# A hybrid trunk of two layers: where the dense blocks and the gates steps of its expert sub-layer are issued

## The chip, the cores and the metric

The kernel runs on one core of a Trainium2 chip. The metric is the device time of one execution in microseconds (us), of which the median over the runs is taken. Within the core, TensorE (PE in the trace, its weight loads PEld) multiplies matrices, VectorE (DVE) and ScalarE (ACT) work on tiles in the on-chip memories, GpSimd (POOL) does the same and issues the gathers of table rows, and SyncE (SP) issues all other transfers. Each engine has its own queue and works it off in order; an instruction waits until what it reads is there and its buffer is free.

## The reference

Two layers over 512 latent tokens and 256 context tokens of width 1024. Each layer is a token mixer (pooling, two kinds of scan, Fourier mixing) and then an expert sub-layer of the PEER kind, each followed by a residual sum and a LayerNorm. Only the expert sub-layer of the latent tokens is touched:

```python
q = (hb @ wq).reshape(t, PEER_HEADS, 2, PEER_DQ // 2)
s = jnp.einsum('thsd,hskd->thsk', q, sub_keys).astype(jnp.float32)
v1, i1 = lax.top_k(s[:, :, 0], PEER_TOPK)
v2, i2 = lax.top_k(s[:, :, 1], PEER_TOPK)
cand = (v1[..., :, None] + v2[..., None, :]).reshape(t, PEER_HEADS, PEER_TOPK * PEER_TOPK)
cid = (i1[..., :, None] * PEER_NKEYS + i2[..., None, :]).reshape(t, PEER_HEADS, PEER_TOPK * PEER_TOPK)
best, pos = lax.top_k(cand, PEER_TOPK)
eid = jnp.take_along_axis(cid, pos, axis=-1)
gate = jax.nn.softmax(best, axis=-1)
act = jax.nn.gelu(jnp.einsum('td,thkd->thk', hb, u_tab[eid]).astype(jnp.float32), approximate=False)
return jnp.einsum('thk,thkd->td', (gate * act).astype(hb.dtype), v_tab[eid])
```

Every token picks 16 of 16384 experts in each of 8 heads by two searches of 16 among 128 keys and one among their sums.

## The kernel before

**Two ways to the same sum.** The 512 latent tokens are four tiles of 128. For tile 3 (`gx`, "the gather") the picked rows of the tables u and v are fetched one per token: 128 turns, each one indirect DMA of 512 KB on POOL's queue (`gat<-in_u`) and one dot product on VectorE (`gat<-gat,hb`), then 128 turns with v, where VectorE adds each row, weighted, to `gacc`. A generator hands out these turns (257 with the last store), and the loops around it decide how many stand beside each piece of other work. It has four `gat` buffers (`GAT = 4`).

For tiles 0 to 2 (`ND = 3`) it is dense: all 16384 experts are applied to all 384 tokens, in 128 chunks of 128 experts, and the results are weighted with a gate matrix that is zero almost everywhere.

**A dense block** (`u_chunk`, L1670) is one chunk of u: SP loads `du` (512 KB), ACT rounds it to `dh`, the remainder `dl` is a subtraction on POOL for chunks below `UN = 48` and on VectorE for the others, TensorE does 24 products of 128x384, ACT takes the Gelu (`da`), and SP stores it to `acts` (192 KB). `du` has three buffers, `dh` and `dl` two. The last 40 chunks are done later, so 88 blocks are handed out by the generator `dense_u`.

**A gates step** (`gates_all`, L1625) makes the gate matrix for 16 tokens; there are 24. VectorE compares `it` (the transposed indices) with a row of numbers (`B`, and `A` twice multiplied with the gate `gp`), TensorE does 32 products `ps<-A,B` a step later, ACT copies them out, partly to `W` and partly through `wst` to DRAM (`rest`, 704 KB).

**The order of the work.** `peer_front` (L1766) computes the scores and searches of all four tiles and then, tile by tile (3, 0, 1, 2), the look-ups: `topk` (L1509) turns positions into expert numbers by comparing and adding up (`oh`, `sel`), all on VectorE. For a dense tile `dense_in` (L1613) has TensorE transpose the two indices and the gate and VectorE store them in `it` and `gp`. Between these pieces `fill` runs dense blocks at a lower priority: one per tile in each of the 8 score units (`FD = 1`, 32 in all) and `FT = 6` behind each tile's look-ups (24). A scheduler then orders each engine's queue by dependences and priority.

After `peer_front` a loop in `run` hands out the other blocks of `dense_u`, each followed by a gates step and `GU` gather turns (2). Then 40 blocks of `dense_uv` (u and v of a chunk together, 2 or 3 gather turns each) and 88 of `dense_v` (6 turns in 7 blocks), then the gather turns that are left and the residuals of the tiles. In layer 0 the context tiles' own gather ends during the look-ups of the latent tiles.

**Lines.** All engine calls go through one recorder, so every instruction has line L149; the tiles' names tell them apart.

Of the kernel before, what the change touches and what calls it, by code (L numbers as in the profile page):

```python
# [50 lines left out]
UN = 48  # L51
VO = 3
DV = 3
FT = 6
UO = 64
FD = 1
GV = (1,1,1,0,1,1,1)
GU = (2,)
GF = (2,3)
GAT = 4  # L60
M1 = ((16,12,9),(18,13,10))
# [122 lines left out]
class K:  # L184
# [1310 lines left out]
    def lookup(self, oh, tab, wide=False):  # L1495


        nc = self.nc
        t = self.oh()
        nc.vector.tensor_tensor(t, oh, tab[:, :, None, :].to_broadcast([128, 8, 16, 16]), op=OP.mult)  # L1500
        o = self.oh((128, 8, 16, 8), F32) if wide else t
        nc.vector.tensor_add(o[:, :, :, :8], t[:, :, :, :8], t[:, :, :, 8:])
        for n in (4, 2):
            nc.vector.tensor_add(o[:, :, :, :n], o[:, :, :, :n], o[:, :, :, n:2 * n])
        e = self.sm((128, 8, 16), "sel", 3)
        nc.vector.tensor_add(e, o[:, :, :, 0], o[:, :, :, 1])
        return e

    def topk(self, tk):  # L1509

        nc = self.nc
        ix, v, best, pos = tk

        gate = self.sm((128, 8, 16), "gate", 2)
        nc.vector.tensor_tensor(gate, best, best[:, :, 0:1].to_broadcast([128, 8, 16]), op=OP.subtract)
        nc.scalar.activation(gate, gate, AF.Exp)
        den = self.t([128, 8], "den", 2)
        nc.vector.tensor_reduce(den, gate, axis=AX.X, op=OP.add)
        nc.vector.reciprocal(den, den)
        nc.vector.tensor_tensor(gate, gate, den[:, :, None].to_broadcast([128, 8, 16]), op=OP.mult)  # L1520

        ib = self.sm((128, 8, 2, 16), "ib", 2, BF)
        nc.vector.tensor_copy(ib, ix)
        pb = self.sm((128, 8, 16), "pb", 2, BF)
        nc.vector.tensor_copy(pb, pos)
        d1 = self.sm((128, 8, 16), "d1", 2, BF)
        nc.vector.tensor_copy(d1[:, :, 0:1], ib[:, :, 0, 0:1])
        nc.vector.tensor_sub(d1[:, :, 1:], ib[:, :, 0, 1:], ib[:, :, 0, :15])
        shape = [128, 8, 16, 16]
        i16, p0, dp = (t[:, None, :].to_broadcast([128, 8, 16]) for t in self.tab)  # L1530
        ge = self.oh()
        nc.vector.tensor_tensor(ge, pb[:, :, :, None].to_broadcast(shape), p0[:, :, None, :].to_broadcast(shape),
                                op=OP.is_ge)
        e1 = self.lookup(ge, d1, True)
        st = self.lookup(ge, dp)
        nc.vector.tensor_sub(pb, pb, st)
        eq = self.oh()
        nc.vector.tensor_tensor(eq, pb[:, :, :, None].to_broadcast(shape), i16[:, :, None, :].to_broadcast(shape),
                                op=OP.is_equal)
        return gate, e1, self.lookup(eq, ib[:, :, 1, :])  # L1540
# [225 lines left out]
    def peer_front(self, l, x, fm, s, h, order, dense=None, n=0, m=0):  # L1766


        NT = len(x)

        self.lo_pool = True
        tk = [self.topk_tiles() for _ in range(NT)]

        def fn(u, S):
            for i in order:
                self.topk_head(u, S[i], tk[i])
                self.fill(n)
        self.peer_scores(l, h, NT, fn)
        self.lo_pool = False
        gg = []  # L1780
        for i in order:
            with self.section() as sec:
                top = self.topk(tk[i])
                if dense is not None and i < ND:
                    self.dense_in(i, top, *dense)
                else:
                    gg.append((i, self.gather_in(l, *top)))
            self.fill(m)
            if gg and (dense is None and len(gg) == NT or dense is not None and len(gg) == 1 and i == gg[0][0]):
                with self.section(sec):  # L1790
                    rows = [self.bcast_row(fm, g, s, 1.0) for g in (3, 4)]
                    gg = [(i, (self.h_tokens(x[i], rows),) + g) for i, g in gg]
        return [g for _, g in gg]

    def run(self):
# [5 lines left out]
        for l in range(L):  # L1801
# [7 lines left out]
            with ExitStack() as mix:  # L1809
# [44 lines left out]
                with self.phase("m2", **(dict(s2=M2X[0], xs2=M2X[1]) if last else dict(s2=M2, s4=3, xs2=M2Y))):  # L1854
# [8 lines left out]
                    late = []  # L1863
# [30 lines left out]
            with self.phase("fx", s2=4, s4=2, x4=2):  # L1894
                self.add(gu)
                gx = self.peer_front(l, x1, fm, 0, hT, (3, 0, 1, 2), (it, gp), FD, FT)
                self.fillers.clear()
            gen = self.gather(l, gx, [accx])
            with self.area("wk", side="right") as wk:

                W = [self.gate_tile(j, wk) for j in range(2)]
                with self.phase("wp"):
                    self.iota = self.t((128, 128, 2), "iota", 1, F16)
                    self.nc.vector.tensor_copy(self.iota, self.iota1[:, :, None].to_broadcast([128, 128, 2]))
                    gs = self.gates_all(it, gp, W, rest)
                    more = True
                    k = 0
                    go = Order(self, UO)
                    while more:
                        with go.main():  # L1910
                            more = next(gu, self) is not self
                        k += 1
                        with go.side():
                            next(gs, None)
                        self.beside(go, GU[k % len(GU)], gen)
                    self.run_all(gs)
                with self.area("vv", side="right") as vv:
                    acc = [[self.pa() if 2 * b + q < PA else self.p() for q in range(2)] for b in range(ND)]
                    go = Order(self, VO)
                    gates = self.gate_blocks(go, W, rest, wk)  # L1920
                    self.dense_uv(l, hT, hu, acc, go, gates, vv, gen)
                    dd.close()

                    def made():
                        if not last:
                            at = self.tc.cur_priority
                            self.tc.cur_priority += RP
                            with self.phase("rc", s2=6, s4=3, ld=3):
                                self.residual(c1, c2, self.spilled(accs), l, fm, 5, 1, 1.0, 2)
                            self.tc.cur_priority = at  # L1930
                    with self.area("aa", side="right") as aa:
                        self.dense_v(l, acts, acc, go, gates, vv, aa, gen, made)
                        self.run_all(gen)
                        with self.phase("rg", s2=6, s4=3, ld=3):
                            self.residual(x1[ND:], x2[ND:], self.spilled([accx]), l, fm, 5, 0, 1.0, 2)
# [133 lines left out]
```

## Time and profile before

| | |
|---|---|
| median of 3 runs | 5824.24 us (5815.28 to 5834.05) |
| the profiled execution | 5827.79 us, its span 5826.0 us |
| busy in the span | TensorE 86%, VectorE 73%, ScalarE 34%, GpSimd 30% |
| mean granted clock of TensorE | 0.928 of full speed |
| moved by DMA | 1372.35 MB, 236 GB/s on average |

Shares of the whole span say little here, since the stages have different limits; what follows reads stretches. A row of a stretch gives its ends, its length, then for PE, PEld, DVE, ACT and POOL the busy us and in brackets the instructions, and last the granted clock of TensorE, the busy share of the DMA engines and GB/s. A timeline row gives start, length, engine, line, operation and what it writes and reads; in square brackets the idle time before it and what ended that.

### The profile page before, as it was taken

To read this page: it belongs to the slowest core of one execution; us is meant where nothing else is said; L and a number is where in the kernel's file an instruction comes from. 1 tells how busy PE (TensorE), PEld (TensorE's weight loads), DVE (VectorE), ACT (ScalarE), POOL (GpSimd) and SP (SyncE) were. 2 spreads that over 40 slices of the span, in tenths; PEclk is the share of its full clock that TensorE was granted. 3 is DMA by queue.
4 is the path that set the end of the run, shared out by engine and by line. 5 is a ranking of instruction groups with operands and counts; after the bars stand their busy time and mean duration, and the time that the engine had idled before them with its cause. 6 is when DMAs were issued, how large, how long until landed. Compare 5 with 4: busy or idle time off the path is not lost. (4 is left out here: it accounts for less than half of the span.)

```text
span 5826.0 us, 76885 instructions
## 1 busy us (share of the span) xinstructions
PE 5023.1 (86%) x26902; PEld 4218.3 (72%) x26902; DVE 4273.4 (73%) x7999; ACT 1954.2 (34%) x3711; POOL 1758.1 (30%) x1290
## 2 busy tenths in 40 slices
PE   8998877987567777889999969999888978899996
PEld 3787755753466677778987858787777977889785
DVE  4665777877788889697777786457565578877778
ACT  2444421321113323343333344333134334433333
POOL 0000344323454675344432220000003443443222
PEclk9998988989679888999999979999998989999998
DMA  6555589878888674699889854433444348988997
GB/s 216 176 164 174 168 300 323 275 271 287 291 273 303 222 241 160 224 313 331 307 311 357 296 190 137 122 111 116 129 132 130 127 133 260 335 293 311 327 327 257
DMA packets 618069, 1372.35 MB, mean 236 GB/s; under 512 B 95568, under 2 KB 229328, under 8 KB 614864
## 3 DMA queue, kind: packets, MB, share of 16 engines
q1 hardware_dynamic: 470224, 830.50, 42.9%
q0 software_dynamic: 147456, 536.94, 27.3%
q8 instruction: 211, 3.46, 0.2%
q14 instruction: 178, 1.46, 0.1%
HBM read 1225.64 MB, written 141.56 MB: 235 GB/s over the span
## 5 line engine op out<-in xcount | busy, mean ns | idle before, releaser
L149 POOL DMA_INDIRECT gat<-in_u,gidx x512 | 680.1, 1328 | 1021.6 <-DVE gat L149 954.7
L149 POOL DMA_INDIRECT gat<-in_v,gidx x512 | 620.2, 1211 | 1020.9 <-DVE gacc L149 893.6
L149 DVE SCALAR_TENSOR_TENSOR gacc<-gat,gact,gacc 128x1024 f32<-128x1024 f32 x508 | 688.5, 1355 | 94.6 <-DMA gat<-in_v,gidx 88.7
L149 DVE SCALAR_TENSOR_TENSOR gat<-gat,hb 128x1024 f32<-128x1024 f32 x512 | 618.9, 1222 | 112.8 <-DMA gat<-in_u,gidx 111.8
L149 PE MATMUL ps<-hx,dh 128*128 128x384 f32 x2304 | 597.6, 339 | 0.0
L149 PE MATMUL ps<-s,s 128*128 128x128 f32 (+3 forms) x2752 | 423.2, 312 | 156.0 <-issue 84.5
L149 PEld LDWEIGHTS ps<-s,s 128*128 128x128 f32 (+1 forms) x2752 | 378.5, 215 | 227.3 <-issue 120.6
L149 PE MATMUL pa<-hx,dh 128*128 128x384 f32 x1792 | 512.4, 356 | 9.4 <-ACT da L149 9.2
L149 ACT CAST dh<-du 128x1024 fp32r<-128x1024 f32 x256 | 268.6, 1050 | 742.0 <-PE ps L149 394.2
L149 DVE TENSOR_TENSOR vl<-dv,vh 128x1024 fp32r<-128x1024 f32 x256 | 313.5, 1225 | 203.3 <-ACT vh L149 198.2
L149 PEld LDWEIGHTS ps<-hx,dh 128*128 128x128 f32 x2304 | 418.0, 189 | 6.9 <-ACT dh L149 1.0
L149 PE MATMUL ps<-hx,dl 128*128 128x384 f32 x1152 | 389.9, 338 | 20.7 <-DVE dl L149 20.7
L149 ACT CAST xwhi<-xwraw 128x512 fp32r<-128x512 f32 x352 | 217.8, 620 | 533.9 <-PE pa L149 414.3
L149 ACT CAST vh<-dv 128x1024 fp32r<-128x1024 f32 x256 | 269.2, 1052 | 341.4 <-PE ps L149 241.4
L149 PE MATMUL pa<-hx,xwhi 128*128 128x512 f32 x1152 | 378.6, 406 | 5.2 <-DVE ld L149 3.1
L149 PE MATMUL ps<-hx,whi 128*128 128x512 f32 x1152 | 381.9, 399 | 0.0
L149 DVE TENSOR_TENSOR xwlo<-xwraw,xwhi 128x512 fp32r<-128x512 f32 x352 | 242.9, 693 | 159.3 <-ACT xwhi L149 144.9
L149 PE MATMUL pa<-hx,dl 128*128 128x384 f32 x896 | 320.6, 358 | 44.5 <-POOL dl L149 44.4
L149 PEld LDWEIGHTS pa<-hx,dh 128*128 128x128 f32 x1792 | 349.6, 202 | 12.6 <-ACT da L149 10.2
L149 ACT CAST whi<-wraw 128x512 fp32r<-128x512 f32 x320 | 197.8, 621 | 474.6 <-PE ps L149 284.7
L149 PE MATMUL ps<-vl,gh 128*128 128x512 f32 x1024 | 317.3, 391 | 0.0
L149 PE MATMUL ps<-vh,gh 128*128 128x512 f32 x1024 | 317.0, 392 | 0.0
(291 smaller groups left out, 11262.3 us busy)
## 6 DMA issues: line engine op xcount, KB each, us to landing
du<-in_ut SPq DMA_DIRECT2D x256, 512.0 KB
dv<-in_v SPq DMA_DIRECT2D x256, 512.0 KB
xwraw<-in_w_in SPq DMA_DIRECT2D x272, 256.0 KB
wraw<-in_w_in SPq DMA_DIRECT2D x176, 256.0 KB
xwraw<-in_w_mod SPq DMA_DIRECT2D x160, 256.0 KB
acts<-da SPq DMA_DIRECT2D x176, 192.0 KB
rest<-wst SPq DMA_DIRECT2D x48, 704.0 KB
W<-rest SPq DMA_DIRECT2D x22, 1536.0 KB
```

The costliest lines, as they stand in the source:

```text
L149: r = f(*a, **kw)
```

## The change

Three numbers and two places in the code:

- `FT` goes from 6 to 1: one dense block instead of six is issued behind each tile's look-ups, so 36 instead of 56 blocks come before the loop and 52 instead of 32 in it.
- `GSK = 2`: in the loop a gates step follows every second block, and `GU = (2,1)`: two and one gather turns alternate.
- In `peer_front` a dense tile's `dense_in` (transposes and stores of `it` and `gp`) is issued one tile later, behind the next tile's look-ups and their block, and for the last tile behind its own. `sel` has six buffers instead of three, `gate` three instead of two.

```diff
--- before.py
+++ after.py
@@ -51,11 +51,12 @@
 UN = 48
 VO = 3
 DV = 3
-FT = 6
+FT = 1
 UO = 64
 FD = 1
 GV = (1,1,1,0,1,1,1)
-GU = (2,)
+GU = (2,1)
+GSK = 2
 GF = (2,3)
 GAT = 4
 M1 = ((16,12,9),(18,13,10))
@@ -1502,7 +1503,7 @@
         nc.vector.tensor_add(o[:, :, :, :8], t[:, :, :, :8], t[:, :, :, 8:])
         for n in (4, 2):
             nc.vector.tensor_add(o[:, :, :, :n], o[:, :, :, :n], o[:, :, :, n:2 * n])
-        e = self.sm((128, 8, 16), "sel", 3)
+        e = self.sm((128, 8, 16), "sel", 6)
         nc.vector.tensor_add(e, o[:, :, :, 0], o[:, :, :, 1])
         return e
 
@@ -1511,7 +1512,7 @@
         nc = self.nc
         ix, v, best, pos = tk
 
-        gate = self.sm((128, 8, 16), "gate", 2)
+        gate = self.sm((128, 8, 16), "gate", 3)
         nc.vector.tensor_tensor(gate, best, best[:, :, 0:1].to_broadcast([128, 8, 16]), op=OP.subtract)
         nc.scalar.activation(gate, gate, AF.Exp)
         den = self.t([128, 8], "den", 2)
@@ -1777,15 +1778,18 @@
                 self.fill(n)
         self.peer_scores(l, h, NT, fn)
         self.lo_pool = False
-        gg = []
+        gg, late = [], []
         for i in order:
             with self.section() as sec:
                 top = self.topk(tk[i])
                 if dense is not None and i < ND:
-                    self.dense_in(i, top, *dense)
+
+                    late.append((i, top))
                 else:
                     gg.append((i, self.gather_in(l, *top)))
             self.fill(m)
+            while late and (late[0][0] != i or i == order[-1]):
+                self.dense_in(*late.pop(0), *dense)
             if gg and (dense is None and len(gg) == NT or dense is not None and len(gg) == 1 and i == gg[0][0]):
                 with self.section(sec):
                     rows = [self.bcast_row(fm, g, s, 1.0) for g in (3, 4)]
@@ -1910,8 +1914,9 @@
                         with go.main():
                             more = next(gu, self) is not self
                         k += 1
-                        with go.side():
-                            next(gs, None)
+                        if k % GSK == 0:
+                            with go.side():
+                                next(gs, None)
                         self.beside(go, GU[k % len(GU)], gen)
                     self.run_all(gs)
                 with self.area("vv", side="right") as vv:
```

VectorE behind the look-ups of layer 1: the last stores of the gate (`gp`), then what follows. Before:

```order
L149 TENSOR_TENSOR gp_37268<-gt_40664,gp_37268 128x128
L149 CAST iota_40883<-iotaf_70 128x256
L149 TENSOR_TENSOR dl_40552<-du_40549,dh_40551 128x1024
...
L149 TENSOR_TENSOR dl_41127<-du_41124,dh_41126 128x1024
L149 TENSOR_TENSOR B_40919<-it_8305_37267,iota_40883 128x2048
L149 TENSOR_TENSOR A_8995_40921<-it_8304_37266,iota_40883 128x2048
```

After:

```order
L150 TENSOR_TENSOR gp_37268<-gt_40188,gp_37268 128x128
L150 CAST iota_40203<-iotaf_70 128x256
L150 SCALAR_TENSOR_TENSOR gat_40240,gdot_40239<-gat_40240,hb_39919 128x1024
L150 TENSOR_TENSOR B_40277<-it_8305_37267,iota_40203 128x2048
L150 TENSOR_TENSOR A_8902_40279<-it_8304_37266,iota_40203 128x2048
L150 TENSOR_TENSOR A_8902_40279<-A_8902_40279,gp_37268 128x2048
L150 SCALAR_TENSOR_TENSOR gat_40283,gdot_40239<-gat_40283,hb_39919 128x1024
L150 TENSOR_TENSOR A_8902_40279<-A_8902_40279,gp_37268 128x2048
```

Before, twelve splits `dl` of dense blocks stand between the last `gp` and the first gates step (`B`, `A`); now a dot (`gat,gdot`) and the step itself come at once.

VectorE inside the loop of layer 1, from one `B` on. Before, one block:

```order
L149 TENSOR_TENSOR B_41158<-it_8305_37267,iota_40883 128x2048
L149 TENSOR_TENSOR A_9033_41160<-it_8304_37266,iota_40883 128x2048
L149 TENSOR_TENSOR dl_41319<-du_41316,dh_41318 128x1024
L149 TENSOR_TENSOR A_9033_41160<-A_9033_41160,gp_37268 128x2048
L149 SCALAR_TENSOR_TENSOR gat_41214,gdot_40925<-gat_41214,hb_40089 128x1024
L149 TENSOR_TENSOR A_9033_41160<-A_9033_41160,gp_37268 128x2048
L149 SCALAR_TENSOR_TENSOR gat_41217,gdot_40925<-gat_41217,hb_40089 128x1024
L149 TENSOR_TENSOR B_41254<-it_8305_37267,iota_40883 128x2048
```

After, one pair of blocks, once the splits are on VectorE (in the first five steps there is no `dl` between them):

```order
L150 TENSOR_TENSOR B_40892<-it_8305_37267,iota_40203 128x2048
L150 TENSOR_TENSOR A_8997_40894<-it_8304_37266,iota_40203 128x2048
L150 TENSOR_TENSOR dl_40994<-du_40991,dh_40993 128x1024
L150 TENSOR_TENSOR A_8997_40894<-A_8997_40894,gp_37268 128x2048
L150 SCALAR_TENSOR_TENSOR gat_40948,gdot_40239<-gat_40948,hb_39919 128x1024
L150 TENSOR_TENSOR A_8997_40894<-A_8997_40894,gp_37268 128x2048
L150 SCALAR_TENSOR_TENSOR gat_40951,gdot_40239<-gat_40951,hb_39919 128x1024
L150 TENSOR_TENSOR dl_41090<-du_41087,dh_41089 128x1024
L150 SCALAR_TENSOR_TENSOR gat_40988,gdot_40239<-gat_40988,hb_39919 128x1024
L150 TENSOR_TENSOR B_41025<-it_8305_37267,iota_40203 128x2048
```

A step's four instructions had one `dl` and two dots beside them, now two `dl` and three dots.

VectorE at the end of layer 1, from the last `vl` of the dense stage on (`hx` is the residual of the dense tiles). Before:

```order
L149 TENSOR_TENSOR vl_49258<-dv_49255,vh_49257 128x1024
L149 SCALAR_TENSOR_TENSOR gacc_45300<-gat_49219,gact_45297,gacc_45300 128x1024
L149 SCALAR_TENSOR_TENSOR gacc_45300<-gat_49284,gact_45297,gacc_45300 128x1024
L149 TENSOR_TENSOR hx_49386<-hx_49386 128x512
L149 SCALAR_TENSOR_TENSOR gacc_45300<-gat_49287,gact_45297,gacc_45300 128x1024
L149 SCALAR_TENSOR_TENSOR hx_49386<-hx_49386 128x512
L149 SCALAR_TENSOR_TENSOR gacc_45300<-gat_49290,gact_45297,gacc_45300 128x1024
L149 BN_STATS hx_49386<-hx_49386 128x6
L149 SCALAR_TENSOR_TENSOR gacc_45300<-gat_49293,gact_45297,gacc_45300 128x1024
```

After:

```order
L150 TENSOR_TENSOR vl_49297<-dv_49294,vh_49296 128x1024
L150 SCALAR_TENSOR_TENSOR gacc_44926<-gat_49258,gact_44923,gacc_44926 128x1024
L150 SCALAR_TENSOR_TENSOR gacc_44926<-gat_49323,gact_44923,gacc_44926 128x1024
L150 TENSOR_TENSOR hx_49386<-hx_49386 128x512
L150 SCALAR_TENSOR_TENSOR gacc_44926<-gat_49326,gact_44923,gacc_44926 128x1024
L150 SCALAR_TENSOR_TENSOR hx_49386<-hx_49386 128x512
L150 TENSOR_TENSOR hx_49386<-hx_49386 128x512
L150 BN_STATS hx_49386<-hx_49386 128x6
L150 SCALAR_TENSOR_TENSOR hx_49386<-hx_49386 128x512
```

Before, `gacc` instructions alternate with the residual, 16 in all behind the last `vl`; now there are three.

## Rows read from the trace of the kernel before

**Rows 1.** stretches of layer 1 (columns as the profile section says)

```profile
4663.00:4763.00 100.00, 71.84 (x364) 69.25 (x364) 96.59 (x127) 30.52 (x41) 45.97 (x16) 0.83 0.37 114
4763.00:4845.00 82.00, 79.58 (x447) 78.59 (x446) 14.44 (x14) 26.96 (x38) 20.66 (x11) 0.98 0.53 174
4845.00:5035.00 190.00, 151.47 (x1304) 143.25 (x1305) 189.45 (x214) 92.46 (x324) 79.53 (x47) 0.96 0.96 303
5035.00:5075.00 40.00, 36.75 (x214) 35.89 (x211) 26.75 (x38) 14.52 (x29) 18.22 (x14) 0.96 1.00 363
5120.00:5390.00 270.00, 270.00 (x1374) 247.14 (x1373) 206.41 (x264) 97.89 (x131) 107.22 (x81) 1.00 0.86 299
...
5779.00:5826.00 47.00, 0.00 (x0) 0.00 (x0) 39.63 (x63) 6.45 (x9) 16.14 (x14) 0.55 0.63 212
```

**Rows 2.** timeline of VectorE: start us, us, engine, line, instruction

```profile
4907.66 1.22 DVE L149 TENSOR_TENSOR B<-it,iota 128x2048 f16<-128x2048 f16 x1
...
4915.63 1.23 DVE L149 TENSOR_TENSOR B<-it,iota 128x2048 f16<-128x2048 f16 x1
```

**Rows 3.** timeline: two Gelus of plain dense blocks, a step's products

```profile
4822.10 0.48 ACT L149 ACTIVATE da<-pa 128x384 f32<-128x384 f32 x1
...
4826.26 0.48 ACT L149 ACTIVATE da<-pa 128x384 f32<-128x384 f32 x1
...
4906.06 2.02 PE L149 MATMUL ps<-A,B 128*128 128x128 f16 x32
```

**Rows 4.** timeline: last gp and 88th Gelu, layer 0 then layer 1

```profile
2375.71 0.28 DVE L149 TENSOR_TENSOR gp<-gt,gp 128x128 f16<-128x128 f32 x1
...
2663.92 0.48 ACT L149 ACTIVATE da<-ps 128x384 f32<-128x384 f32 x1
...
4762.86 0.29 DVE L149 TENSOR_TENSOR gp<-gt,gp 128x128 f16<-128x128 f32 x1
...
5070.07 0.48 ACT L149 ACTIVATE da<-ps 128x384 f32<-128x384 f32 x1
```

**Rows 5.** DMA queues in 4850:5030, 4763:4840, 2640:2700: packets, MB, share

```profile
q0 software_dynamic: 6494, 23.66, 42.6%
q1 hardware_dynamic: 37576, 30.96, 52.9%
...
q1 hardware_dynamic: 4651, 11.71, 47.2%
...
q0 software_dynamic: 3170, 11.53, 50.8%
q1 hardware_dynamic: 3958, 10.58, 48.7%
```

**Rows 6.** timeline of VectorE in the look-ups: one instruction, twice

```profile
4703.48 2.28 DVE L149 TENSOR_TENSOR oh<-pb,tab 128x2048 bf16<-128x2048 bf16 x1
...
4709.98 4.48 DVE L149 TENSOR_TENSOR oh<-pb,tab 128x2048 bf16<-128x2048 bf16 x1
```

**Rows 7.** splits dl in layer 0's look-ups: PE, PEld, DVE, POOL, clock, DMA

```profile
2250.00:2376.00 126.00, 52.84 (x138) 30.18 (x139) 0.00 (x0) 45.65 (x18) 0.85 0.51 168
```

**Rows 8.** waits of TensorE in layer 1's look-ups: us, times, longest

```profile
PE ps L149 <- DVE sel L149: 18.6, 3, 7.2
```

**Rows 9.** timeline of VectorE at the end of layer 1

```profile
5776.81 1.28 DVE L149 SCALAR_TENSOR_TENSOR gacc<-gat,gact,gacc 128x1024 f32<-128x1024 f32 x1
5778.00 0.69 DVE L149 SCALAR_TENSOR_TENSOR hx<-hx 128x512 f32<-128x512 f32 x1
...
5802.29 1.28 DVE L149 SCALAR_TENSOR_TENSOR gacc<-gat,gact,gacc 128x1024 f32<-128x1024 f32 x1 [1.72 <-DMA gat<-in_v,gidx]
```

**Rows 10.** waits between 3375 and 3440, the end of layer 0

```profile
PE ps L149 <- DVE la L149: 22.1, 1, 22.1
...
DVE gacc L149 <- DMA gat<-in_v,gidx: 3.8, 3, 1.6
```

**Rows 11.** waits in the gates stage of layer 1

```profile
PE ps L149 <- DVE A L149: 34.2, 20, 7.5
```

## The prediction

> **What bounds the kernel now.** I read the stretches of layer 1's expert sub-layer first [rows 1], then looked into each with the timeline. The stretch 4663 to 4763 is the look-ups: VectorE is busy 96.59 of 100 us, TensorE 71.84 at a granted clock of 0.83. From 4763 to 4845 it is reversed: TensorE runs dense blocks nearly without a gap (79.58 of 82) and VectorE is busy 14.44. From 4845 to 5035 come the 24 gates steps: VectorE 189.45 of 190, TensorE 151.47. Then eight dense blocks, and from 5075 on the two long stages; in the first of them TensorE is busy 270.00 of 270, so what happens beside it costs nothing. The front of this sub-layer is thus bound by VectorE, TensorE and VectorE again, in turn; a balanced mixture would be shorter. Layer 0 has the same shape.
>
> A gates step sits in one dense block, and VectorE's period is 4915.63 - 4907.66 = 7.97 us [rows 2]: seven instructions (comparison B, comparison A, two products, the split dl, two dots of gathered rows) at 1.14 us each. On TensorE a dense block takes 4826.26 - 4822.10 = 4.16 us when nothing holds it, and a step's 32 products 2.02 us [rows 3]; 6.18 of 7.97 us are used.
>
> The stage that I compare runs from the last gp instruction (the last tile's gate is ready) to the Gelu of the 88th block: 2663.92 - 2375.71 = 288.2 us in layer 0 and 5070.07 - 4762.86 = 307.2 us in layer 1 [rows 4].
>
> **The stage after the change.** Dense blocks issued in the front fall from 32 + 24 to 32 + 4, so 52 of 88 are left for the gates loop, not 32. By the order, TensorE runs four of them behind the last transposes and then 24 times two blocks and one step. The four take 4 x 4.16 = 16.6 us; VectorE goes straight on to the first step, so that it is ready by then. The 80 us of dense work that ran beside an idle VectorE are now the cover of the steps. Per pair of blocks:
> TensorE needs 2 x 4.16 + 2.02 = 10.3 us. VectorE needs four gates instructions, three dots, two splits: 9 x 1.14 = 10.3 us. They tie, where VectorE was 1.8 us longer in every block.
> The DMA engines are the unknown, for the gathers per step rise from two to three and the chunks from one to two. In the gates stage queue q0 took 42.6% of 180 us for 23.66 MB, 45 gathers of 0.524 MB: 1.70 us each; q1 took 52.9% for 30.96 MB, which at 1.442 MB a block (chunk 0.524, acts 0.197, gates to DRAM 0.721) is 21.5 blocks, 4.43 us each [rows 5]. Before it, without gates, q1 took 47.2% of 77 us for 11.71 MB, 16.2 blocks of chunk and acts: 2.24 us each; so the gates store costs 2.19. A pair is then 2 x 2.24 + 2.19 + 3 x 1.70 = 11.8 us. But such prices stretch with the load: where the engines were driven hardest (2640 to 2700), q0 took 50.8% of 60 us for 11.53 MB, 22 gathers, 1.39 us each, and q1 48.7% for 10.58 MB, 2.76 us per MB or 1.99 for chunk and acts; the pair is then 2 x 1.99 + 2.19 + 3 x 1.39 = 10.3 us. I take 11.0, the middle of 10.3 and 11.8, since no row has this mixture.
>
> The first four pairs differ. Chunks below 48 have their split on POOL; 40 are through when the first step runs, so in eight blocks POOL's splits now run beside gates steps. In the look-ups a VectorE instruction that takes 2.28 us took 4.48 beside such a split [rows 6], 2.20 more. VectorE then needs 7 x 1.14 + 2 x 2.20 = 12.4 us per pair. The bound below is 11.0 (they don't meet), above 7 x 1.14 + 2 x 2.54 = 13.1 (each split stops VectorE for all of its mean time, 45.65/18 [rows 7]); I take 12.4.
> The Trainium skill (SBUF — State Buffer, section "Who interferes with whom") says that a VectorE instruction with two SBUF inputs and a GpSimd one that reads SBUF exclude each other for a whole instruction. The 4.48 us agree; no run here shows a gates step beside a split. By that rule the upper bound holds, and the result would be 6 us later over both layers.
>
> Stage: 16.6 + 4 x 12.4 + 20 x 11.0 = 286.2 us.
>
> **When the stage starts.** In layer 1 the order has 15.5 dense blocks from the end of the searches to the last transposes, before 18.8. That takes about three POOL splits out of the look-ups, each 2.2 us of VectorE, so they end 6 us sooner. In layer 0 it is 7.2 blocks fewer, of the 18 splits in its 126 us [rows 7]: 15 us; and the order moves 8 of the context tiles' last gathers (1.2 us each) from the look-ups behind them, 9 us sooner, but ten of them now stand before or among the first steps, 12 us later. That TensorE does less during the look-ups is counted already, since those blocks are among the 52. The waits that the later transposes aim at, 18.6 us in three pieces [rows 8], go only in part: the order still has tile 0's first transpose behind the same ten blocks. They lie in a stretch that VectorE ends, so they are worth nothing by themselves; six `sel` buffers and three `gate` buffers cost no instruction.
> Layer 0: 288.2 + 24 - 12 - 286.2 = 14 us gained. Layer 1: 307.2 + 6 - 286.2 = 27 us. Together 41.
>
> **The ends of both layers.** The tail tile's gather has 257 turns. Before: 64 beside the gates loop, 100 and 75 beside the two long stages, 18 behind them. Now 52 x 1.5 = 78, so 4 are left. The order puts 3 gacc behind the last vl of layer 1 where 16 stood, and 2 for 16 in layer 0. In layer 1 TensorE has nothing left at 5779, and 47 us follow [rows 1]. There a gacc holds VectorE for 1.19 us (5776.81 to 5778.00), with waits for rows, the longest 1.72 [rows 9], of 3.4 us in all; nearly every VectorE instruction there is on the path to the output. 13 x 1.19 + 3.4 = 18.9 us at most; I take 18, not below 12. In layer 0 TensorE stands until la, in the end 22.1 us at a stretch; the gathers' waits for rows are 3.8 us [rows 10]. 14 x 1.19 + 3.8 = 20.5 us go at most; some hops between ACT, POOL and TensorE on the way to la stay, and next on the path are weight loads queued on SP behind the residual's stores, which move with it. I take 15, not below 8. Together 33.
> The 14 gathers don't vanish: they are in the three dots of each pair, counted above. The long stages have the same turns as before, and TensorE fills them.
>
> **Sum.** 41 + 33 = 74. The profiled execution took 5827.8 us (span 5826.0, 1.8 around it), so 5753.8; the median of the runs is 5824.24, 3.5 below it: 5750 us.
>
> **Rivals.** (a) DMA hides: every pair at TensorE's 10.3 us, stage 264; layer 0 gains 36, layer 1 49, the ends 33: 118, 5706. For it: the 363 GB/s of 5035 to 5075 [rows 1] are what (1.573 + 1.049 + 0.393 + 0.721) MB in 10.3 us need. Against: that stretch had no gates store. Chance 0.12.
> (b) DMA becomes the bound, 11.8 us per pair or above. At 11.8 the stage is 16.6 + 4 x 12.4 + 20 x 11.8 = 302, layer 0 loses 2, layer 1 gains 11, the ends 33: 42, 5782; at 12.6, 5814. For it: the engines are 0.96 busy in the stage already. Against: TensorE's waits there ended with VectorE's A, 34.2 us in 20 [rows 11], not with a landing. Chance 0.19, of which 0.05 lie within 0.3% of the time before.
> (c) Slower: POOL's queue is in order, and in the first part of the loop each split stands between gathers that wait for one of four `gat` buffers; a buffer comes free by a dot, the dot stands on VectorE behind a product that waits for an A buffer, that for TensorE's step, and that for a split. If this closes into a ring, the times add up: 8.3 of blocks, 2.0 of products, 5.1 of splits, 8.0 of VectorE, 23 us a pair. Four pairs in two layers lose 8 x (23 - 12.4) = 85 us: 5835. It decides from 21.7 us a pair on (12.4 + 74/8). Against: four buffers are more than the three gathers of a pair. Chance 0.05.
> (d) The forecast, 5725 to 5780: 0.64.
>
> **Numbers.** (a) reaches 5706, a few us less if the ends give their most; (b) 5814, (c) 5835. 8 times in 10: 5712 to 5808. A change under 0.3% (17.5 us) can't be told from none in this kernel. Faster: 0.64 + 0.12 + 0.14 from (b) = 0.90, less 0.02 for a milder (c) beside the forecast: 0.88. Same 0.05 + 0.02 = 0.07, slower 0.05.
>
> **What would show it.** Right: no stretch of dense blocks beside an idle VectorE behind the look-ups; B instructions 10.5 to 11.5 us apart, with TensorE and VectorE both over 90% busy; 3 gacc behind the last vl; la some 15 us sooner behind layer 0's last V block; 29 us, not 47, from TensorE's last product to the end. Wrong: B over 12.5 us apart with dots waiting for landings (b); TensorE released by POOL's dl in the first pairs after gaps over 5 us (c); or its clock at 1.2 GHz (a granted 0.5) in the loop, which would double the 4.16 us.

## The result and the profile after

The changed kernel took 5739.1 us (median of 4 runs, 5736.66 to 5742.45); the kernel before took 5820.77 us on the same chip (4 runs). The ratio is 0.9849, 95% interval 0.9835 to 0.9863: 1.5% faster. The forecast was 5750 us, so the direction and the range held and the time was 11 us too high. By the medians 81.7 us are gained. The profiled executions lie further apart: the one after has a span of 5734.9 us, 91.1 less than before, where the forecast gave 74.

Stretches of layer 1's expert sub-layer, which answer to [rows 1] (same columns): the look-ups, the four dense blocks behind them, the first pairs of the gates loop, the other pairs, the first long stage, and what follows TensorE's last product.

```profile
4620.00:4710.00 90.00, 57.97 (x283) 55.98 (x283) 88.74 (x125) 25.60 (x35) 39.16 (x12) 0.77 0.33 103
4710.00:4728.30 18.30, 17.40 (x94) 17.08 (x93) 4.24 (x3) 5.31 (x8) 10.95 (x7) 0.93 0.45 151
4728.30:4789.00 60.70, 45.72 (x321) 44.62 (x322) 42.08 (x45) 22.14 (x66) 37.24 (x21) 0.86 0.76 248
4789.00:5000.00 211.00, 208.11 (x1604) 205.10 (x1604) 205.30 (x242) 106.76 (x321) 103.76 (x62) 0.98 1.02 363
5060.00:5320.00 260.00, 260.00 (x1321) 237.71 (x1320) 199.24 (x239) 94.32 (x127) 103.22 (x79) 1.00 0.85 297
5705.50:5735.00 29.50, 0.00 (x0) 0.00 (x0) 23.78 (x50) 6.22 (x9) 3.07 (x4) 0.56 0.40 138
```

The 82 us in which TensorE ran dense blocks beside an idle VectorE have shrunk to 18.3. Behind the first pairs both engines are busy (208.11 and 205.30 of 211). But from 4728 to 4789, in the first pairs, neither is: 45.72 and 42.08 of 60.7. TensorE's last product is now followed by 29.5 us, not 47.

Two steps of the steady part, which answer to [rows 2]; the period is 10.25 us for a pair of blocks.

```profile
4907.94 1.22 DVE L150 TENSOR_TENSOR B<-it,iota 128x2048 f16<-128x2048 f16 x1
4918.19 1.22 DVE L150 TENSOR_TENSOR B<-it,iota 128x2048 f16<-128x2048 f16 x1
```

The last gp and the 88th Gelu of both layers, which answer to [rows 4], then the end of layer 0 (the last split vl and la, for which TensorE waits) and of layer 1 (the last vl and the gacc behind it).

```profile
2344.87 0.28 DVE L150 TENSOR_TENSOR gp<-gt,gp 128x128 f16<-128x128 f32 x1
...
2637.30 0.48 ACT L150 ACTIVATE da<-ps 128x384 f32<-128x384 f32 x1
...
3353.10 1.23 DVE L150 TENSOR_TENSOR vl<-dv,vh 128x1024 fp32r<-128x1024 f32 x1 [0.72 <-ACT vh L150]
...
3396.49 0.19 DVE L150 SCALAR_TENSOR_TENSOR la<-dt,row 128x48 f32<-128x48 f32 x1
3396.73 2.75 PE L150 MATMUL ps<-la,masks 128*128 128x24 f32 x12 [17.11 <-DVE la L150]
...
4709.86 0.29 DVE L150 TENSOR_TENSOR gp<-gt,gp 128x128 f16<-128x128 f32 x1
...
5000.27 0.48 ACT L150 ACTIVATE da<-ps 128x384 f32<-128x384 f32 x1
...
5697.77 1.22 DVE L150 TENSOR_TENSOR vl<-dv,vh 128x1024 fp32r<-128x1024 f32 x1 [0.72 <-ACT vh L150]
5698.92 2.60 DVE L150 SCALAR_TENSOR_TENSOR gacc<-gat,gact,gacc 128x1024 f32<-128x1024 f32 x2
...
5703.09 1.28 DVE L150 SCALAR_TENSOR_TENSOR gacc<-gat,gact,gacc 128x1024 f32<-128x1024 f32 x1
```

The stage is 292.4 us in layer 0 and 290.4 in layer 1, against 288.2 and 307.2. Piece by piece, from the starts of such instructions in both traces (us gained; "last search" is the last MAX8 over the scores, `tkv<-sc`):

| piece | forecast | measured |
|---|---|---|
| layer 0, last search to last gp (133.6 to 105.3) | 24 | 28.3 |
| layer 0, last gp to 88th Gelu, with 12 for context gathers | -10 | -4.2 |
| layer 0, last vl to la (62.6 to 43.4) | 15 | 19.2 |
| layer 1, last search to last gp (104.7 to 95.3) | 6 | 9.4 |
| layer 1, last gp to 88th Gelu | 21 | 16.8 |
| layer 1, last vl to the end (54.5 to 37.1) | 18 | 17.4 |
| all other stretches | 0 | 4.2 |
| sum | 74 | 91.1 |

The last line but one is small against what these stretches do by themselves: in the kernels below (best1 apart), whose code ahead of layer 0's searches is the same, these begin anywhere from 1984 to 2006 us.

### The profile page after: what moved, and what is told of

The parts are those of the page before. It is cut to its first block, busy times and chain, and to the rows that moved or that the text cites. A ratio compares the mean times of both kernels' runs of the same rounds, so it can differ in the third digit from the quotient of the medians.

```text
span 5734.9 us, 76857 instructions
## 1 busy us (share of the span) xinstructions
PE 5001.5 (87%) x26902; PEld 4212.1 (73%) x26902; DVE 4267.5 (74%) x7999; ACT 1951.3 (34%) x3711; POOL 1771.4 (31%) x1290
## 3 DMA queue, kind: packets, MB, share of 16 engines
q8 instruction: 211, 3.46, 0.2%
## 4 chain that ended last, share of the span: by engine, by line
PE 55%; DVE 12%; DMA 10%; issue 9%; POOL 5%; ACT 2%; SPq 0%; POOLq 0%; DVEq 0%; ACTq 0%
PE ps L150 39%; PE pa L150 16%; POOL gat L150 4%; DVE s L150 3%; DMA gat<-in_v,gidx 3%; DMA gat<-in_u,gidx 2%; DVE oh L150 1%; DVE gacc L150 1%; DVE gat L150 1%; DMA dv<-in_v 1%; DMA wraw<-in_w_out 1%; POOL dl L150 1%; DMA a<-acts 1%; DMA wraw<-in_w_in 1%; DVE tki L150 1%
## 5 line engine op out<-in xcount | busy, mean ns | idle before, releaser
L150 PE MATMUL ps<-hx,dh 128*128 128x384 f32 x2944 | 758.8, 338 | 0.0
L150 PEld LDWEIGHTS ps<-hx,dh 128*128 128x128 f32 x2944 | 534.9, 190 | 5.8
L150 PE MATMUL ps<-hx,dl 128*128 128x384 f32 x1472 | 495.7, 337 | 2.7 <-POOL dl L150 2.6
L150 PE MATMUL pa<-hx,dh 128*128 128x384 f32 x1152 | 343.3, 362 | 7.5 <-ACT da L150 7.3
L150 PE MATMUL ps<-vh,gl 128*128 128x512 f32 x1024 | 316.1, 390 | 0.0
L150 POOL TENSOR_TENSOR dl<-du,dh 128x1024 fp32r<-128x1024 f32 x96 | 250.5, 2611 | 200.5 <-ACT dh L150 183.9
```

Source lines behind the costliest of these rows:

```text
L150: r = f(*a, **kw)
```

## Where the first pairs lose their time

In the steady part a pair takes 10.25 us. The first five pairs, by the Gelus of their blocks, take 77.5 us together in layer 1 (20.9, 10.2, 19.4, 10.2, 16.7) and 79.7 in layer 0. The waits of 4728.3 to 4789 (engine, what waits, what ended the wait: us, times, longest; the wait of 14.1 us ended just ahead of this stretch):

```profile
DVE gat L150 <- DMA gat<-in_u,gidx: 30.7, 4, 14.1
POOL dl L150 <- ACT dh L150: 18.1, 5, 8.0
PE ps L150 <- DVE A L150: 15.1, 4, 6.7
...
ACT dh L150 <- POOL dl L150: 10.9, 4, 2.7
```

And the timeline, rows of VectorE, TensorE and POOL put in order of time:

```profile
4715.95 2.39 POOL L150 TENSOR_TENSOR dl<-du,dh 128x1024 fp32r<-128x1024 f32 x1 [23.89 <-ACT dh L150]
4718.50 1.02 POOL L150 DMA_INDIRECT gat<-in_u,gidx  x1 [0.16 <-issue]
...
4724.41 3.97 DVE L150 SCALAR_TENSOR_TENSOR gat<-gat,hb 128x1024 f32<-128x1024 f32 x1 [14.06 <-DMA gat<-in_u,gidx]
...
4734.12 0.27 PE L150 MATMUL ps<-A,B 128*128 128x128 f16 x1 [6.72 <-DVE A L150]
...
4745.14 2.69 POOL L150 TENSOR_TENSOR dl<-du,dh 128x1024 fp32r<-128x1024 f32 x1 [7.98 <-ACT dh L150]
...
4747.98 0.96 POOL L150 DMA_INDIRECT gat<-in_u,gidx  x1
4749.30 2.40 POOL L150 TENSOR_TENSOR dl<-du,dh 128x1024 fp32r<-128x1024 f32 x1 [0.36 <-ACT dh L150]
...
4753.65 1.22 DVE L150 SCALAR_TENSOR_TENSOR gat<-gat,hb 128x1024 f32<-128x1024 f32 x1 [8.05 <-DMA gat<-in_u,gidx]
...
4765.10 3.46 PE L150 MATMUL ps<-A,B 128*128 128x128 f16 x31 [4.19 <-DVE A L150]
```

Each engine waits for the next. POOL, in order, holds a gather behind a split that waits 7.98 us for its rounded chunk dh. VectorE, in order, holds the next comparison behind the dot of that gather (8.05 us). TensorE waits for the product A behind that comparison. A new dh buffer comes free when TensorE has run a block: the profile puts ACT's waits down to POOL's dl, but those dl had ended, and beside plain blocks the roundings start 4.16 us apart, which is TensorE's block. By the reading of these rows this is a ring over POOL, VectorE and TensorE, as in rival (c), with ACT's rounding between. Its links are not all those of (c), where the gathers wait for buffers: here POOL waits for buffers once, 1.8 us, and for dh 18.1 us. The very first gather of the tail tile stood in the same way behind a split that had waited 23.89 us for dh, and VectorE waited 14.06 us for it.

The waits have a second price. Two steps behind such a wait of TensorE, read as stretches:

```profile
4736.40:4739.90 3.50, 3.50 (x32) 3.50 (x32) 3.50 (x6) 2.17 (x9) 0.76 (x1) 0.52 0.60 190
4765.10:4768.60 3.50, 3.50 (x32) 3.50 (x32) 3.45 (x6) 2.17 (x10) 1.90 (x1) 0.50 0.80 265
```

The granted clock is 0.52 and 0.50 there, the lower of its two levels (1.2 of 2.4 GHz), and 31 products of a step take 3.46 us, where 32 took 2.02 [rows 3]. Layer 1 has three such steps. That is some 5 us (an estimate, 3 x 1.7) of the 26 us by which its first five pairs exceed five pairs of 10.25.

The runs below test the ring (theory 1) against two other theories: that POOL's splits only stop VectorE while they run (theory 2), and that the first pairs are slow for a reason of their own (theory 3).

## The experiments

All were timed beside the kernel before on the same chip; the ratios, with their 95% intervals, are to it. Its median was 5820.8 to 5832.2 us on the four occasions, so times in us compare to within some 10 us from one chip to another, and the ratios compare better.

**The changed kernel again** (rep), on the chip of a, b and c below. 

> The changed kernel once more, unchanged, on the chip of a, b and c, so that they are compared with it directly: 5739 us, within 6.


Measured 5736.82 us, ratio 0.9832 (0.9813 to 0.9852): the result stands.

**The mixture taken out** (gsk1):

```
-GSK = 2
+GSK = 1
```

> The changed kernel with a gates step beside every block of the loop, not every second; all else of the change stays. If the gain comes from the mixture (one step to two blocks lets TensorE and VectorE tie at 10.3 us), the stage falls apart again into 24 blocks bound by VectorE at 7.4 to 8 us and 28 blocks at TensorE's 4.16 us: 2 x 4.16 + 24 x 7.7 + 28 x 4.16 = 309 us where 291 stand now, about 5775 us. If the gain comes from the blocks moved out of the look-ups, the later transposes or the gathers' turns, it stays: 5739.


Measured 5809.98 us, ratio 0.9978 (0.9967 to 0.9989): 1.3% of the 1.5% is gone, so the gain needs the mixture. The whole loss lies in the stage, which is 335.0 and 330.5 us in the two layers, where the changed kernel has 292.4 and 290.4; the ends of the layers stay as short as there (37.1 us from the last vl to the end). The 309 us worked out left out the slow first pairs: the first ten blocks take 28 and 19 us more than ten later ones with steps (74.6 us), and the changed kernel's lose 28 and 26 against its own pace of 10.25 us a pair. So the difference of some 40 us a layer is the mixture's.

**The front and the loop as before** (ft6); only the later transposes and the buffers of sel and gate are left:

```
-FT = 1
+FT = 6
-GU = (2,1)
+GU = (2,)
-GSK = 2
+GSK = 1
```

> The change without its mixture: six dense blocks behind each tile's look-ups, a gates step beside every block, two gather turns beside each, as before; only the transposes one tile later and the longer life of sel and gate are left. If these are worth nothing by themselves: 5825, the time before. Rival: a part of the gain is theirs, 5790 to 5810.


Measured 5820.31 us, ratio 0.9981 (0.9969 to 0.9992). From the last search to the 88th Gelu it is 3.7 us shorter than before in layer 0 and 3.2 in layer 1: what is left of the change is worth 0.2%, no more. Within that, layer 0's look-ups end 16.8 us sooner, and the stage behind them is 13.0 us longer.

**Transposes right behind their look-ups again** (late):

```
-late.append((i, top))
+self.dense_in(i, top, *dense)
```

> The changed kernel with each tile's transposes issued right behind its look-ups again, as before; all else of the change stays. The prediction held the later transposes to be worth nothing by themselves, since their waits lie in a stretch that VectorE ends: 5739 us, within 5. Rival: the 18.6 us of TensorE's waits for sel per layer were on the path, and come back: up to 5776.


Measured 5754.65 us, ratio 0.9869 (0.9853 to 0.9884): 0.2% above the changed kernel, with intervals that overlap. In layer 1's look-ups TensorE waits for sel for 31.0 us, in the changed kernel for 29.2 and before for 18.6 [rows 8], so the later place spares hardly any wait there. In layer 0's it spares 14.9 us (44.7 against 29.8); the look-ups end 15.0 us sooner by it, of which the stage behind gives back 8.3. From the last search to the 88th Gelu layer 1 takes 385.4 us, as the changed kernel (385.7). Layer 0 takes 404.3 against 397.7, and 399.9 in rep. So the later transposes give nothing in layer 1 and 4 to 7 us in layer 0. Most of the rest lies ahead of layer 0's searches (1999.5 us against 1987.6), a stretch that the edit doesn't touch.

**What bounds a steady pair.** One gather turn beside a block (gu1):

```
-GU = (2,1)
+GU = (1,)
```

> The changed kernel with one gather turn beside each block of the loop: two to a pair, 52 in all, so that 30 and not 4 are left behind the last block. If TensorE's 2 x 4.16 + 2.02 = 10.3 us bind a steady pair, it stays at 10.25 us although VectorE then needs 9.1 and the DMA engines move 14% less; the 26 gathers more at each end cost 1.4 us each (gu0: 16.8 us for 12), 73 us: 5812. If VectorE or the DMA engines bind it, a pair falls to 9.1 to 9.5 us, up to 55 us come back: 5757 to 5770.


Every store of gates twice (st2; the line that makes the tensor `again` is left out here):

```
+nc.sync.dma_start(self.again[:, :, g].rearrange("m p x -> p m x"), st.rearrange(...))
```

> The changed kernel with every store of gates to DRAM issued twice, the second time into a tensor that nothing reads: 0.72 MB more in each pair of about 3.73 MB. If the DMA engines are at their limit in the steady pairs (the profile shows a share of 1.04 at 362 GB/s), a pair stretches to 10.25 x 4.45 / 3.73 = 12.2 us, 24 pairs in two layers, 94 us: 5833. If they have slack that the share doesn't show, pairs stay at 10.25 us: 5739 to 5745.


The steady stretch of gu1, and that of st2:

```profile
4830.00:4960.00 130.00, 130.00 (x1023) 127.96 (x1023) 118.14 (x129) 67.92 (x207) 43.37 (x26) 1.00 0.99 319
```

```profile
4840.00:5010.00 170.00, 158.04 (x1200) 154.36 (x1199) 152.72 (x179) 78.51 (x238) 74.95 (x46) 0.98 1.07 386
```

The longest wait of ACT in that stretch of st2:

```profile
ACT dh L150 <- DMA du<-in_ut: 64.8, 19, 6.1
```

In gu1 a pair still takes 10.24 us in both layers, though VectorE is 91% busy and DMA moves 319 GB/s: TensorE, 130 of 130 us busy, binds it. In the changed kernel VectorE's sum ties with it, as forecast. In st2 a pair takes 11.6 us in layer 0 and 11.5 in layer 1, not the 12.2 of engines at their limit: they gave 386 GB/s instead of the 363 of the changed kernel, and then held the loop, for the roundings wait 64.8 of 170 us for landings of chunks, where in the changed kernel's steady pairs none of these waits appears. So a DMA share of 1.02 was not yet the limit, and it was near. st2 took 5798.61 us, ratio 0.9951 (0.9937 to 0.9965), 34 less than the full stretch; gu1 5801.4, ratio 0.9952 (0.9937 to 0.9966). gu1 leaves 29 gacc behind the last vl, and 77.4 us from it to the end of layer 1, where the changed kernel has 3 and 37.1: 1.55 us each.

**The splits of the first pairs on VectorE** (un40):

```
-UN = 48
+UN = 40
```

> The splits dl of the blocks from 40 on, not 48, go to VectorE, so that none stands on POOL in the first pairs of the gates loop of the changed kernel (there the first four pairs take 68.4 us in layer 0 and 55.3 us in layer 1, where four later ones take 41.0). Theory 1 (a ring through POOL's queue: gathers wait behind splits that wait for TensorE's blocks, which wait for products, which wait on VectorE for the dots of those gathers): the first pairs come down to about 10.3 us, with the context gathers of layer 0 some 13: 14 us gained in layer 1, 15 in layer 0, about 5710 us. Theory 2 (a split on POOL stops VectorE for its own time, and that is all): 2.2 us a split less 1.14 us for the split that VectorE gets instead, 8 splits in two layers, 17 us, about 5722. Theory 3 (the first pairs are slow for another reason, as the lower clock or the start of the stream): no change, 5739.


Measured 5724.25 us, ratio 0.9823 (0.9806 to 0.9839). Its first 80 us behind the last gp, in layer 0 and in layer 1:

```profile
2353.20:2433.20 80.00, 53.98 (x360) 51.64 (x359) 59.30 (x64) 23.77 (x63) 42.98 (x27) 0.83 0.83 267
4714.10:4794.10 80.00, 75.25 (x514) 73.32 (x513) 62.27 (x74) 32.47 (x88) 39.03 (x24) 0.91 0.85 288
```

And those of the changed kernel:

```profile
2344.90:2424.90 80.00, 59.99 (x389) 57.97 (x388) 59.38 (x56) 26.93 (x70) 60.08 (x34) 0.85 0.84 271
4709.90:4789.90 80.00, 63.22 (x415) 61.80 (x415) 46.85 (x48) 27.93 (x72) 48.19 (x27) 0.88 0.69 227
```

The time alone fits theory 2 (5722), but it is made up of other parts. Layer 1's stage falls by 16.0 us, from 290.4 to 274.4: theory 1 said 14, theory 2 half of 17. Layer 0's stays at 293.4, and there theory 1 as I had put it fell. TensorE now waits there for a split on VectorE:

```profile
2414.98 0.69 PE L150 MATMUL ps<-hx,dl 128*128 128x384 f32 x1 [16.33 <-DVE dl L150]
```

By the timeline that split stands on VectorE behind dots of the tail tile, whose gathers POOL issues behind the last context gathers. The place in the ring had only been changed.

**No gathers beside the first eight blocks, splits left on POOL** (gu0):

```
-GU = (2,1)
+GU = (2,) + (0,) * 8 + (2,) + (2,1) * 21
```

> The changed kernel, its splits on POOL as they are, but no gather turn beside the first eight blocks of the gates loop; 67 turns, not 78, so that 15 are left behind the last block instead of 4. Theory 1 (ring): with no gathers among POOL's splits the first four steps follow one another at 10.3 to 12.4 us a pair, though the splits stay; about 29 us gained less some 8 for the splits' own hold on VectorE, and 11 gathers more at the end of each layer at 1.2 us, 26: 5744 us. Theory 2 (POOL's splits stop VectorE): the first pairs stay at 14 to 17 us less the three dots of 1.14 where VectorE was full; about 5760. Theory 3: first pairs unchanged, 5765.


Measured 5729.84 us, ratio 0.985 (0.9834 to 0.9866). The stage is 278.4 us in layer 0 and 271.7 in layer 1. By the Gelus the first four pairs of layer 1 take 10.24 us each; the fifth, when the gathers come back, takes 17.7. The first 80 us again, in both layers:

```profile
2341.90:2421.90 80.00, 68.24 (x465) 66.25 (x464) 66.82 (x52) 31.39 (x86) 51.60 (x28) 0.91 0.83 266
4704.10:4784.10 80.00, 74.31 (x538) 73.04 (x537) 51.33 (x49) 35.17 (x100) 43.62 (x22) 0.94 0.72 230
```

Two rows of a comparison A, one beside a split:

```profile
4705.81 1.22 DVE L150 TENSOR_TENSOR A<-it,iota 128x2048 f16<-128x2048 f16 x1
...
4710.34 2.59 POOL L150 TENSOR_TENSOR dl<-du,dh 128x1024 fp32r<-128x1024 f32 x1 [23.98 <-ACT dh L150]
4710.60 3.41 DVE L150 TENSOR_TENSOR A<-it,iota 128x2048 f16<-128x2048 f16 x1
```

The split does hold VectorE: the comparison takes 3.41 us instead of 1.22, longer by about the time that was left of the split. The Trainium skill (SBUF — State Buffer, section "Who interferes with whom") says that a VectorE instruction with two SBUF inputs contends with a GpSimd instruction that reads SBUF; this trace agrees. But with those splits where they were, layer 1's stage is as short as un40's, since VectorE has room there (51.33 of 80 us busy). Theories 2 and 3 fall: either taking the splits off POOL (un40) or taking the gathers away (gu0) shortens layer 1's stage, so it is the two together on POOL's queue that cost the time. The gain was given back at the ends: 15 gacc behind the last vl, 53.9 us from it to the end of layer 1, not 37.1.

**That given back, got again** (a, gu0 with a gather turn beside every block of the last stage):

```
-GV = (1,1,1,0,1,1,1)
+GV = (1,)
```

> gu0 (no gather turn beside the first eight blocks of the loop, splits left on POOL) with a gather turn beside every block of the last stage: 13 turns more there, so 2 and not 15 are left. If the turns cost nothing in the last stage, which TensorE fills, the stretch from the last vl to the end falls from 53.9 us to about 36 us in layer 1 and as much in layer 0, where gu0 gave back what its front gained: 5730 - 2 x 17 = 5696 us. Rival: 13 turns more lengthen the last stage (372 us), 1.2 us each, and nothing is gained: 5725 to 5730.


Measured 5710.99 us, ratio 0.9796 (0.9777 to 0.9816). From the last vl to the end of layer 1 are 38.6 us (36 expected), and the stage ahead of it takes 374.1, not 372.0: the turns cost 2 us there, not 15. The time is 15 us above the 5696 expected; layer 0's searches begin 14 us later than in gu0 (1998.4 against 1984.1), in a stretch that the edit doesn't touch.

**un40 with the same turns, and with the context gathers put ahead** (best1):

```
-GV = (1,1,1,0,1,1,1)
+GV = (1,)
-GP = 3000
+GP = 1500
```

> Splits of the blocks from 40 on VectorE (as un40), the context gathers of layer 0 put ahead (their priority offset 1500, not 3000: 27 of them stand among the searches, none behind the last gp), and a gather turn beside every block of the last stage (GV of ones: none is left behind the last vl). Theory 1 (layer 0's first pairs wait for the context gathers): the stretch from last gp to the 88th Gelu falls from 293 us (un40) to 275 in layer 0, as it stands in layer 1; the searches before it get longer by 0 us (they fit into VectorE's idle 16% there) to 32 us (27 x 1.2). Rival: layer 0's first pairs are slow for their own reason, 290 us stay. The ends: 37 us from the last vl to the end of layer 1 now; at least 5 us less in each layer (three gacc), up to 15 if the gathered tile's residual also goes beside the V blocks. Together 5724 - 18 - 2 x 10 = 5686 us, 5670 to 5720.


Measured 5730.32 us, ratio 0.9823 (0.9809 to 0.9838). The first half came: layer 0's stage is 274.6 us. The second did not: the searches, from first to last, take 267.6 us instead of 251.3, and begin at 2023 us, 17 later than in any other kernel here. The context gathers did not fit in: 16 us were paid in the searches, and 17 more ahead of them if those are the priority's price too, for 19 in the stage and 6 in the look-ups.

**un40 with the turns alone** (b): 

> un40 (splits of the blocks from 40 on VectorE) with a gather turn beside every block of the last stage, and the context gathers where they were: best1 without its priority offset. best1's ends were 8.3 us (layer 1) and 12.6 us (layer 0) shorter than un40's, while its searches in layer 0 were about 43 us longer. If that was the price of the context gathers put ahead, it is gone here: 5724 - 21 = 5703 us, layer 0's first pairs slow again (293 us from last gp to the 88th Gelu). Rival: the searches were longer by disturbance, and the 19 us that best1 won in layer 0's first pairs are lost: 5740.


Measured 5713.76 us, ratio 0.9795 (0.9775 to 0.9816). Layer 0's searches take 250.8 us again and its stage 291.8: the priority's price is gone, and so is what it won. From the last vl to the end of layer 1 are 28.8 us, and to la in layer 0 39.6. The time is 11 us above the 5703 expected. Most of that is the gain of 12.6 us at layer 0's end, of which 1.1 came: from its last vl to the searches of layer 1 are 1070.0 us, in un40 1071.1, in best1 1058.5.

**b without gathers beside the first four blocks** (c):

```
-GU = (2,1)
+GU = (2,) + (0,) * 4 + (1,2) * 23 + (1,)
```

> b, and no gather turn beside the first four blocks of the loop (72 turns, not 78): the context gathers of layer 0 then share VectorE and POOL with no gather of the tail tile, and VectorE has room for them (two dots of the first pairs gone). Theory 1 (the ring is the tail tile's gathers behind POOL's work and the context gathers): from last gp to the 88th Gelu 293 falls to about 279 in layer 0 and 274 to 271 in layer 1, 5703 - 17 = 5686 us. Rival (the context gathers alone cost it): layer 0 stays at 290, 5700.


Measured 5683.95 us, ratio 0.9742 (0.9723 to 0.9762), against rep's 0.9832 on the same chip: 0.9% below the changed kernel and 2.6% below the one before. The first 80 us behind the last gp of either layer:

```profile
2362.70:2442.70 80.00, 75.07 (x546) 73.30 (x546) 77.80 (x81) 36.73 (x102) 47.97 (x28) 0.98 0.98 343
4694.20:4774.20 80.00, 80.00 (x596) 78.90 (x595) 67.92 (x77) 37.48 (x104) 35.47 (x22) 0.98 0.88 304
```

TensorE has no gap in layer 1: the stage is 264.1 us, where 52 blocks of 4.16 us and 24 steps of 2.02 make 264.8. Layer 0 comes to 267.9 with all its context gathers where they were, so these alone were not the cause; they cost when the tail tile's gathers stood behind them. The 5686 us expected came.

## Why the prediction was right, and where its terms were not

- **What bounds the kernel, and what the mixture does: right.** gsk1 and ft6 show that nearly all of the gain needs one step to two blocks. But 36.6 of the 91.1 us lie at the ends of the layers, and gsk1 keeps these: they come from the gather turns moved into the loop, where the mixture makes room for them. Run a shows that turns beside the last stage cost next to nothing; whether the kernel before could have had the ends that way, without the mixture, was not run.
- **The steady pair, "I take 11.0": too high.** It is 10.25 us, the pair of rival (a), and just outside the 10.5 to 11.5 that were named as the sign. TensorE binds it (gu1); the DMA engines had some slack above their share of 1.02 (st2). The price per MB taken under light load (11.8 a pair) was the wrong end of the two; the one taken under the heaviest load (10.3) came close. 19 pairs at 0.76 us: 14.4 us a layer for the better.
- **The first pairs, "7 x 1.14 + 2 x 2.20 = 12.4": too low.** The five first pairs of layer 1 took 77.5 us where the forecast has 4 x 12.4 + 11.0 = 60.6. The term counted VectorE's time beside a split; that hold is real (3.41 us for 1.22), but un40 and gu0 show that the wait was the ring's. The forecast knew a ring, as rival (c), and gave it 23 us a pair or nothing. It came at some 15.5 on average: every second pair took 17 to 21 us, the ones between them 10.2. Its reason against, that four gather buffers are more than a pair's three gathers, failed: the gathers are held by POOL's order, not by buffers. And its sign, TensorE released by POOL's dl, named the wrong link: TensorE was released by VectorE's A, after gaps of up to 6.72 us.
- **The two errors stand against each other.** In layer 1: 16.9 us lost in the first pairs, 14.4 won in the others, 1.8 lost in front of them, so that the stage was 4.2 us longer than 286.2. That they cancel is luck: the time was forecast better than its terms.
- **"VectorE goes straight on to the first step": wrong.** It waited 14.06 us for the first gather, whose dot stands ahead of the comparison, and that gather stood on POOL behind a split; the four blocks ran beside an idle VectorE.
- **The start of the stage and the ends: right in kind.** 28.3 and 9.4 us for 24 and 6; 17.4 for 18 in layer 1. Layer 0's end gave 19.2, where 20.5 had been worked out as the most and 15 taken; that the hops on the way to la were hardly on the path is an inference. But layer 0's 28.3 us are not those of the forecast: with the transposes back in their place (late) the look-ups gain 13.4, so the splits and context gathers, which were to give 24, gave no more than that, and the later transposes gave the rest.
- **The 12 us for ten context gathers among layer 0's first steps: too many.** Layer 0's stage is 2.0 us longer than layer 1's; the ring held both.
- **Later transposes "worth nothing by themselves": right in layer 1, off by 4 to 7 us in layer 0** (late).
- Rivals (b) and (c) as results did not come. The granted clock was 0.86 on average in layer 1's first pairs and 0.98 in the others. The lower level, named as a sign of being wrong, did show, in the step behind each long wait of TensorE, and not in the steady pairs.

## What to carry to other kernels

When work is moved so that two engines balance, look at the first steps of the mixture apart from the steady ones: engines with in-order queues can lock into a ring there that averages don't show. Here it was opened by taking a link out: the gathers in both layers, the splits in one. The work taken out cost little once it had another place beside the engine that binds (2 us for 13 turns). A unit price read from a lightly loaded stretch overstated here what the loaded one paid; take the price from the busiest stretch, then ask with one run whether the resource has any more to give.

## What the runs showed of the hardware

A mean DMA share of 1.02 at 363 GB/s was not the ceiling: with more to move the same engines gave 386 GB/s at 1.07, and there the transfers lengthened the loop (11.5 us a pair for 10.25). The share is no measure of slack by itself. A VectorE instruction with two inputs in SBUF took 3.41 us for 1.22 beside a POOL split, and this cost nothing where VectorE had room. Behind waits of TensorE of 6.7 and 4.2 us the granted clock was 0.5 for the step that followed, whose products took 3.5 us and not 2.02; it was 1.00 in the blocks behind that step.
